# A two-layer trunk on one core: the dt chain moved to GpSimd, earlier tables, an opening with ones-matmuls, a split last half row

## The chip, the cores and the metric

One NeuronCore of one Trainium2 chip runs the whole program; the other cores are idle. The metric is the device time of one execution, in microseconds. The kernel before takes 1440.32 us (median of 3 runs, 1438.73 to 1442.22).

## The reference, cut to what matters

512 tokens of width 1024, float32, two layers. Each layer is a token mixer and a gated ConvFFN, both followed by a LayerNorm of `alpha*x + f(x)`. The mixer of layer 0 is a Mamba-2 scan, that of layer 1 a chunked spatial gate. The change touches the beginning of the scan and the very last LayerNorm:

```
zxbcdt = x @ w_in;  z, xbc, dt = split(zxbcdt)
xbc = silu(causal_dwconv(xbc));  xs, B, C = split(xbc)          # 8 groups, 4 heads each
dt = softplus(dt + dt_bias);  A = -exp(a_log);  Acum = cumsum(dt*A)
y_diag = sum_j (C_i.B_j) exp(Acum_i - Acum_j) dt_j x_j          # j <= i
states = sum_j B_j exp(Acum_last - Acum_j) dt_j x_j
out = layer_norm(alpha*x + conv_ffn(x))                         # the end of layer 1
```

## The kernel before, in words

Every float32 product is made of three matmuls in a rounded format: each operand is split into a rounded high part (a cast on ScalarE, ACT) and a low part (a subtraction on VectorE, DVE); the products high-high, high-low and low-high are summed in PSUM. The weights are one list `wall` of 244 tiles of 128x1024; `w_prep` (L74 to L85) loads each over the SP queue, casts it (L80) and subtracts (L82), six tiles ahead of its use. A projection tile of 128 channels by 512 tokens takes 24 matmuls of 512 columns, `mm_k` (L123 to L128), three for each of 8 blocks k of 128 input channels.

**Opening (L102 to L147).** The loop goes over k in pairs. For each k it loads a 256 KB block of x transposed (L136), casts it (L137) and subtracts (L138); for each pair it loads 256 columns of the first two weight tiles in 128 KB pieces (`w_piece`, L107 to L112); then it issues six matmuls, three into each of `ps_b[0]` and `ps_b[1]`, the first two channel tiles. That is 16 transfers. After them come `wdt` and the parameter table `ppt` (L144, L145) and the dt projection `dt_mm` into `ps_dt` (L119).

**The dt chain (L342 to L363).** One 128x128 tile (4 token blocks by 32 heads on the partitions, 128 tokens along the row) goes through the softplus by a polynomial, the product with exp(a_log), and a running sum S (the scan, L357). ACT does the exponentials, DVE the rest, one dependent instruction after another. S is written to DRAM (`scr`, L359) and read back broadcast to all partitions, for one group of four heads at a time (`R`, L377). `dt_cols` (L365 to L369) transposes three results on TensorE (PE) into `ptdt` and copies them to `tcol`; it is called when the matmuls of projection tile j=4, the first of group 1, have been issued.

**A group (L374 to L456).** `ssd(g, cv)` is a generator; `advance` (L460) calls its next part at each projection tile. Its first part loads R, issues the products C.B into `pcb`, the transposes of B (`pb`) and of x (`px`) on PE, then on ACT the decay tables `cd`, `E` (16 Relu, one Exp) and `EB`, and after them the copy `btok` of the transposed B (L409). Its second part issues the state products `pst` (L429), which read `btok`. For group 0 the first part is called after tile j=6 and the second after j=7.

**The end (`out_proj`, from L205).** The output projection sums 22 k-blocks into eight banks `acc[t][h]` (four row tiles t, two halves h of 512 columns). The last 5 k-blocks are done row tile by row tile (`tail`, half by half), so that each row tile's LayerNorm (`stats`, L252) runs while the next one's matmuls do. In `stats` DVE adds the residual (L259), takes the sums of 512 columns (L260) for each half, merges them (L261); GpSimd (POOL) takes the power -1/2 (L203); DVE scales, and SP writes out.

**What sets the order.** Instructions are written in the order of the source, each engine runs its own queue in a fixed order, and a planner (Tile) lays out the queues ahead of time by dependencies, priorities and a cost estimate, and puts in the semaphores. `tc.high_priority()` puts what is inside ahead. A queue stops at its first instruction that has to wait. PSUM has eight banks (`pst`).

Of the kernel before, what the change touches and what calls it, by code (L numbers as in the profile page):

```python
# [14 lines left out]
P = 128  # L15
T = 512
# [33 lines left out]
LOOK = 6  # L50


@with_exitstack
def trunk_kernel(ctx, tc, x_tok, x_t, w_dt, wall, pp, ln_g, ln_b, b_v, b_s, w_s_t, out):
# [52 lines left out]
    def w_piece(i, q):  # L107
        raw, hi, lo = first[i]
        cs = slice(q * 256, (q + 1) * 256)
# [20 lines left out]
    with tc.tile_pool(name="xload", bufs=8) as xl:  # L130
        wdt = xl.tile([P, NK, 32], F32, name="wdt", bufs=1)
        xr = []
        for q in range(4):
            for k in (2 * q, 2 * q + 1):
                xr.append(xl.tile([P, T], F32, tag="xr", name=f"xr{k}"))
                nc.sync.dma_start(xr[k], x_t[:, k, :])  # L136
                nc.scalar.copy(xT_hi[:, k, :], xr[k])  # L137
                nc.vector.tensor_sub(xT_lo[:, k, :], xr[k], xT_hi[:, k, :].bitcast(F32))  # L138
                if k % 2 == 0:
                    w_piece(0, q)  # L140
                    w_piece(1, q)
                for ps, f in zip(ps_b, first):
                    mm_k(ps, f[1:], k, 0, T)
# [61 lines left out]
    def out_proj(lnp, split, base, nk, ln, last, hooks=None, nxt=None, mid=None):  # L205
# [4 lines left out]
        def mm(t, h, k, a, w):  # L210
            o = acc[t][h]
            ts_ = slice(t * P, (t + 1) * P)
            hs = slice(h * T, (h + 1) * T)
            nc.tensor.matmul(o, a[0][:, ts_], w[0][:, hs], start=(k == 0), stop=False)  # L214
            nc.tensor.matmul(o, a[0][:, ts_], w[1][:, hs], start=False, stop=False)  # L215
            nc.tensor.matmul(o, a[1][:, ts_], w[0][:, hs], start=False, stop=(k == nk - 1))  # L216
# [28 lines left out]
        def tail(t):  # L245
            order = [(h, k) for h in range(2) for k in range(nm, nk)]
            if t == NT - 1 and not last:
                order = [(h, k) for k in range(nm, nk) for h in range(2)]
            for h, k in order:
                mm(t, h, k, *aw[k - nm])  # L250

        def stats(t):  # L252
            r = lnp.tile([P, D], F32, tag="r", bufs=2, name=f"r{base}_{t}")
            st = block(lnp, 12, f"st{base}_{t}", "st", 2).rearrange("p (a b) -> p a b", a=2)
# [70 lines left out]
    with ExitStack() as st:  # L325
# [16 lines left out]
        nc.scalar.activation(v, ps_dt[:, 0:P], AF.Identity, bias=col(C_DT))  # L342
        nc.vector.scalar_tensor_tensor(u, v, -1.0, v, ALU.mult, ALU.min)
        nc.scalar.activation(u, u, AF.Exp)
        nc.scalar.activation(ea, col(C_DT + 1), AF.Exp)
        nc.vector.tensor_scalar_add(q, u, 2.0)
        nc.vector.reciprocal(q, q)
        nc.vector.tensor_mul(u, u, q)
        nc.vector.tensor_mul(s2, u, u)
        nc.vector.tensor_scalar_mul(q, s2, 1.0 / 13.0)  # L350
        for c in (11, 9, 7, 5, 3):
            nc.vector.scalar_tensor_tensor(q, q, 1.0 / c, s2, ALU.add, ALU.mult)
        nc.vector.scalar_tensor_tensor(q, q, 1.0, u, ALU.add, ALU.mult)
        nc.vector.tensor_scalar_max(v, v, 0.0)
        nc.vector.scalar_tensor_tensor(v, q, 2.0, v, ALU.mult, ALU.add)
        nc.vector.tensor_scalar_mul(u, v, ea)
        nc.vector.tensor_tensor_scan(S, ones, u, 0.0, ALU.mult, ALU.add)  # L357
        for c in range(NT):
            nc.sync.dma_start(scr[:, c * P:(c + 1) * P], S[32 * c:32 * c + 32, :])  # L359
        nc.vector.tensor_scalar_mul(nsl, S[:, P - 1:P], -1.0)  # L360
        nc.scalar.activation(t4, S, AF.Exp, bias=nsl)
        nc.vector.tensor_mul(t4, t4, v)
        nc.vector.tensor_scalar_mul(u, S, -1.0)  # L363
# [10 lines left out]
        def ssd(g, cv):  # L374
            Bt, Ct, x0, x1 = (cv[:, i, :] for i in range(4))
# [4 lines left out]
            cd = small[:, 32 + 16 * (g % 2):48 + 16 * (g % 2)].rearrange("p (h c) -> p h c", h=4)  # L380
            pcb = pst(f"pcb{g}")
# [15 lines left out]
            nc.scalar.activation(cd, R[:, :, P - 1::P], AF.Exp, scale=-1.0)  # L397
            E = gp.tile([P, NT, 4, P], F32, tag="E", bufs=1, name=f"E{g}")
            for c in range(NT):
                for h in range(4):  # L400
                    nc.scalar.activation(
                        E[:, c, h, :], R[:, h, c * P:(c + 1) * P], AF.Relu,
                        bias=tcol[:, 0, c, 4 * g + h:4 * g + h + 1])
            nc.scalar.activation(E, E, AF.Exp, scale=-1.0)
            for h in range(2):
                hs = slice(64 * h, 64 * h + 64)
                nc.scalar.activation(EB[hs], R[hs, h::2, P:], AF.Exp, scale=-1.0)
# [353 lines left out]
```

## Time and profile before

| | |
|---|---|
| median of 3 runs | 1440.32 us |
| the profiled execution's own time | 1439.39 us |
| its span (first to last instruction) | 1437.5 us |
| PE busy | 1423.6 us (99%), 6911 matmuls and transposes |
| DVE, ACT, POOL busy | 846.1, 611.5, 23.7 us |
| DMA | 152.66 MB, mean 106 GB/s |

Times in the rows are from the start of the span. The span and the execution's time differ by 1.9 us, and the profiled execution is 0.9 us under the median. A matmul's row shows a modelled end, longer than the distance to the next one's start; the pace of a stream is the distance between starts.

### The profile page before, as it was taken

The page shows a single profiled execution, that of the slowest core. Times are in us where ns is not written, and L with a number is a line of the kernel's source. Part 1 is how long each engine was busy: PE and PEld are TensorE (multiplying, and loading weights), DVE is VectorE, ACT ScalarE, POOL GpSimd, SP SyncE. Part 2 cuts the span into 40 slices and gives each one's busy share as a digit, 9 for nine tenths or more (in the row PEclk, how much of TensorE's full clock was granted, in tenths as well). Part 3 has the DMA queues.
Part 4 walks back from the last instruction along what each step waited for, and adds up shares of the span by engine and source line. Part 5 has one row for each costly group of instructions (what it writes and reads, how often), then busy time and mean ns, then how long its engine had stood idle before and what let it go on. Part 6 is the DMA issues. An engine that isn't in the chain of part 4 may idle for free.

```text
span 1437.5 us, 17317 instructions
## 1 busy us (share of the span) xinstructions
PE 1423.6 (99%) x6911; PEld 1187.8 (83%) x6911; DVE 846.1 (59%) x1147; ACT 611.5 (43%) x893; POOL 23.7 (2%) x30
## 2 busy tenths in 40 slices
PE   8999999999999999999999999999999999999997
PEld 6788888888889888888888888888888888888886
DVE  6878777565378655554336556446378655554336
ACT  5886677343245433333233433223255433333220
POOL 0000000000000000000000000000000000000001
PEclk9999999999999999999999999999999999999999
DMA  6533322333424332323331432223223333333311
GB/s 219 206 106 129 106 100 74 88 115 122 160 73 123 112 99 92 103 90 101 93 98 59 154 125 88 88 88 118 89 81 127 101 103 93 98 103 118 103 44 59
DMA packets 42864, 152.66 MB, mean 106 GB/s; under 512 B 4760, under 2 KB 6040, under 8 KB 41504
## 3 DMA queue, kind: packets, MB, share of 16 engines
q1 hardware_dynamic: 40240, 143.17, 31.0%
q10 hardware_dynamic: 2544, 8.39, 1.7%
q8 instruction: 54, 0.88, 0.2%
q14 instruction: 26, 0.21, 0.0%
HBM read 149.37 MB, written 2.18 MB: 105 GB/s over the span
## 4 chain that ended last, share of the span: by engine, by line
PE 96%; ACT 1%; DVE 1%; DMA 1%; issue 0%; SPq 0%; DVEq 0%; ACTq 0%
PE ip L126 18%; PE ip L127 18%; PE ip L128 18%; PE acc L216 10%; PE acc L214 10%; PE acc L215 10%; PE pv L576 2%; PE pv L578 2%; PE pv L577 2%; PE psp L636 1%; PE py L443 1%; PE pt L279 1%; PE po L450 1%; PE pst L429 1%; PE pcb L384 0%; PE px L395 0%
## 5 line engine op out<-in xcount | busy, mean ns | idle before, releaser
L126 PE MATMUL ip<-xT_hi,whi 128*128 128x512 f32 (+1 forms) x1264 | 484.4, 383 | 0.0
L128 PE MATMUL ip<-xT_hi,wlo 128*128 128x512 f32 (+1 forms) x1264 | 479.8, 380 | 0.0
L127 PE MATMUL ip<-xT_lo,whi 128*128 128x512 f32 (+1 forms) x1264 | 478.7, 379 | 0.0
L82 DVE TENSOR_TENSOR wlo<-wraw,whi 128x1024 fp32r<-128x1024 f32 x242 | 295.7, 1223 | 297.8 <-ACT whi L80 297.3
L80 ACT CAST whi<-wraw 128x1024 fp32r<-128x1024 f32 x242 | 253.8, 1051 | 355.8 <-PE ip L127 289.3
L126 PEld LDWEIGHTS ip<-xT_hi,whi 128*128 128x128 f32 x1264 | 237.9, 188 | 45.3 <-issue 1.2
L128 PEld LDWEIGHTS ip<-xT_hi,wlo 128*128 128x128 f32 x1264 | 237.7, 188 | 44.6
L127 PEld LDWEIGHTS ip<-xT_lo,whi 128*128 128x128 f32 x1264 | 238.0, 188 | 43.3 <-issue 0.2
L214 PE MATMUL acc<-whi,ahi 128*128 128x512 f32 x608 | 237.3, 390 | 0.0
L216 PE MATMUL acc<-whi,alo 128*128 128x512 f32 x608 | 236.6, 389 | 0.0
L215 PE MATMUL acc<-wlo,ahi 128*128 128x512 f32 x608 | 236.5, 389 | 0.0
L214 PEld LDWEIGHTS acc<-whi,ahi 128*128 128x128 f32 x608 | 114.1, 188 | 24.2 <-issue 0.8
L216 PEld LDWEIGHTS acc<-whi,alo 128*128 128x128 f32 x608 | 114.1, 188 | 23.7
L215 PEld LDWEIGHTS acc<-wlo,ahi 128*128 128x128 f32 x608 | 114.1, 188 | 23.6
L193 DVE TENSOR_TENSOR alo<-h,ahi 128x512 fp32r<-128x512 f32 x44 | 30.4, 691 | 103.4 <-ACT ahi L192 103.4
L192 ACT CAST ahi<-h 128x512 fp32r<-128x512 f32 x44 | 27.4, 623 | 141.7 <-PE acc L215 119.5
L180 DVE SCALAR_TENSOR_TENSOR cv<-ip,ppt,cv 128x511 f32<-128x511 f32 (+2 forms) x90 | 66.9, 744 | 2.0 <-ACT cv L178 1.9
L180 DVE SCALAR_TENSOR_TENSOR gt<-ip,ppt,gt 128x511 f32<-128x511 f32 x88 | 65.7, 746 | 1.6 <-ACT gt L178 0.3
L180 DVE SCALAR_TENSOR_TENSOR ut<-ip,ppt,ut 128x511 f32<-128x511 f32 x88 | 65.7, 746 | 1.3
L563 ACT ACTIVATE gt<-gt 128x512 f32<-128x512 f32 x44 | 27.8, 632 | 82.6 <-DVE gt L180 82.5
L284 ACT ACTIVATE xf<-pt,ppt 128x128 f32<-128x128 f32 x96 | 36.6, 466 | 46.0 <-PE pt L279 43.6
L576 PE MATMUL pv<-whi,xT_hi 128*128 128x512 f32 x128 | 50.0, 390 | 0.0
(138 smaller groups left out, 1073.9 us busy)
## 6 DMA issues: line engine op xcount, KB each, us to landing
wraw<-in_wall_dram SPq DMA_DIRECT2D x242, 512.0 KB
xres<-scr SPq DMA_DIRECT2D x8, 1024.0 KB
xr<-in_x_t_dram SPq DMA_DIRECT2D x8, 256.0 KB
xres<-rscr SPq DMA_DIRECT2D x2, 1024.0 KB
xres<-in_x_tok_dram ACTq DMA_DIRECT2D x1, 2048.0 KB
out_dram<-r SPq DMA_DIRECT2D x8, 256.0 KB
wraw_s<-in_wall_dram SPq DMA_DIRECT2D x8, 128.0 KB
lngf<-in_ln_g_dram ACTq DMA_DIRECT2D x2, 512.0 KB
```

What stands on the lines that cost most here:

```text
L80: nc.scalar.copy(hi, raw)
L82: nc.vector.tensor_sub(lo, raw, hi.bitcast(F32))
L126: nc.tensor.matmul(o, whi[:, cs], xT_hi[:, k, lo:hi], start=(k == 0), stop=False)
L127: nc.tensor.matmul(o, whi[:, cs], xT_lo[:, k, lo:hi], start=False, stop=False)
L128: nc.tensor.matmul(o, wlo[:, cs], xT_hi[:, k, lo:hi], start=False, stop=(k == NK - 1))
L180: nc.vector.scalar_tensor_tensor(o[:, s:], ps[:, :T - s], col(c + taps - 1 - s), o[:, s:], ALU.mult, ALU.add)
L193: nc.vector.tensor_sub(lo, self.act(k), hi.bitcast(F32))
L214: nc.tensor.matmul(o, a[0][:, ts_], w[0][:, hs], start=(k == 0), stop=False)
L215: nc.tensor.matmul(o, a[0][:, ts_], w[1][:, hs], start=False, stop=False)
L216: nc.tensor.matmul(o, a[1][:, ts_], w[0][:, hs], start=False, stop=(k == nk - 1))
L284: nc.scalar.activation(xf[:, q, :], pt[:, q * P:(q + 1) * P], AF.Identity, scale=col(c), bias=col(c + 8))
L576: nc.tensor.matmul(ps, xT_hi[:, k, ts_], whi, start=(k == 0), stop=False)
```

## The change

- **Ones-matmuls.** Seven matmuls of the 128x128 tile of ones with itself, into `ps_dt`, stand ahead of the opening. Nothing reads their result.
- **Opening.** x arrives as blocks 0 and 1 (256 KB each) and then three pairs of 512 KB; the first two weight tiles come in pieces of 256, 256 and 512 columns. 11 transfers in place of 16, the same bytes.
- **dt chain.** 17 instructions leave DVE; 18 on POOL lead to the scan and three follow it. The reciprocal and the scan stay on DVE. The first exponent is now `exp(-|.|)` on ACT from PSUM. All of it has high priority.
- **Tables.** `decay(g)`, the load of R and the tables, is a function; for group 0 it is called right after `dt_cols`. In `ssd` the copy `btok` stands ahead of the tables.
- **Last half row.** For the last row tile of the last projection, half h=1 is computed as two pieces of 256 columns (30 matmuls in place of 15), and its residual and sums are taken in two pieces; the sums of this row tile are all taken over 256 columns.

```diff
+WARM = 7
+    pieces = {0: slice(0, 256), 2: slice(256, 512), 4: slice(512, 1024)}
+    for i in range(WARM):
+        nc.tensor.matmul(ps_dt[:, 0:P], ones, ones, start=True, stop=True)
...
+        xall = xl.tile([P, NK, T], F32, name="xall", bufs=1)
+        for k in range(NK):
+            xr.append(xall[:, k, :])
+            if k < 2:
                 nc.sync.dma_start(xr[k], x_t[:, k, :])
+            elif k % 2 == 0:
+                nc.sync.dma_start(xall[:, k:k + 2, :], x_t[:, k:k + 2, :])
+            nc.scalar.copy(xT_hi[:, k, :], xr[k])
+            nc.vector.tensor_sub(xT_lo[:, k, :], xr[k], xT_hi[:, k, :].bitcast(F32))
+            if k in pieces:
+                for i in range(2):
+                    w_piece(i, pieces[k])
+            for ps, f in zip(ps_b, first):
+                mm_k(ps, f[1:], k, 0, T)
...
+            if t == NT - 1 and last:
+                for h, c0, c1 in ((0, 0, 512), (1, 0, 256), (1, 256, 512)):
+                    for k in range(nm, nk):
+                        mm(t, h, k, *aw[k - nm], c0, c1)
+                return
...
             for h in range(2):
-                nc.vector.scalar_tensor_tensor(r[:, hs], xres[:, t, hs], ALPHA, acc[t][h], ALU.mult, ALU.add)
-                nc.vector.bn_stats(st[:, h, :], r[:, hs])
+                for c in ((0, 256) if short and h else (0,)):
+                    n = T // 2 if short and h else T
+                    nc.vector.scalar_tensor_tensor(
+                        r[:, h * T + c:h * T + c + n], xres[:, t, h * T + c:h * T + c + n], ALPHA,
+                        acc[t][h][:, c:c + n], ALU.mult, ALU.add)
+                    if short:
+                        for b in range(c // 256, (c + n) // 256):
+                            nc.vector.bn_stats(st[:, 2 * h + b, :], r[:, h * T + 256 * b:h * T + 256 * b + 256])
...
+        with tc.high_priority():
+            nc.scalar.activation(u, ps_dt[:, 0:P], AF.Abs, bias=col(C_DT))
+            nc.scalar.activation(u, u, AF.Exp, scale=-1.0)
+            nc.scalar.activation(v, ps_dt[:, 0:P], AF.Identity, bias=col(C_DT))
+            nc.scalar.activation(ea, col(C_DT + 1), AF.Exp)
+            gs.tensor_scalar_add(q, u, 2.0)
+            nc.vector.reciprocal(q, q)
+            gs.tensor_scalar_max(v, v, 0.0)
+            gs.tensor_tensor(u, u, q, ALU.mult)
+            gs.tensor_tensor(s2, u, u, ALU.mult)
+            gs.tensor_scalar(q, s2, 1.0 / 13.0, 1.0 / 11.0, ALU.mult, ALU.add)
+            for c in (9, 7, 5, 3):
+                gs.tensor_tensor(q, q, s2, ALU.mult)
+                gs.tensor_scalar_add(q, q, 1.0 / c)
+            gs.tensor_tensor(q, q, s2, ALU.mult)
+            gs.tensor_scalar(q, q, 1.0, 2.0, ALU.add, ALU.mult)
+            gs.tensor_tensor(q, q, u, ALU.mult)
+            gs.tensor_tensor(v, v, q, ALU.add)
+            gs.tensor_scalar_mul(u, v, ea)
+            nc.vector.tensor_tensor_scan(S, ones, u, 0.0, ALU.mult, ALU.add)
...
+            gs.tensor_scalar_mul(nsl, S[:, P - 1:P], -1.0)
+            nc.scalar.activation(t4, S, AF.Exp, bias=nsl)
+            gs.tensor_scalar_mul(u, S, -1.0)
+            gs.tensor_tensor(t4, t4, v, ALU.mult)
...
             btok = gp.tile([P, 3, P], F32, tag="btok", bufs=1, name=f"btok{g}")
             nc.scalar.copy(btok, pb[:, 0:384].rearrange("p (c n) -> p c n", c=3))
+            EB, cd, E = decays.pop(g) if g in decays else decay(g)
...
                 if g == 1 and k == 0:
                     dt_cols()
+                    decays[0] = decay(0)
```

## Rows read from the trace of the kernel before

**Rows 1.** The page's part 4: who holds the chain that ended last.
```profile
PE 96%; ACT 1%; DVE 1%; DMA 1%; issue 0%; SPq 0%; DVEq 0%; ACTq 0%
```
**Rows 2.** Waits of PE, whole run: who waited for whom, us, times, longest.
```profile
PE pst L429 <- ACT btok L409: 0.6, 1, 0.6
PE ptdt L368 <- DVE xres L363: 0.5, 1, 0.5
```
**Rows 3.** Timeline of PE's opening: start, us, instruction [idle before <-releaser].
```profile
4.71 0.80 PE L126 MATMUL ps_b<-xT_hi,whi_s 128*128 128x512 f32 x1 [4.71 <-ACT whi_s L111]
8.12 0.80 PE L126 MATMUL ps_b<-xT_hi,whi_s 128*128 128x512 f32 x1 [0.49 <-ACT xT_hi L137]
9.44 0.63 PE L128 MATMUL ps_b<-xT_hi,wlo_s 128*128 128x512 f32 x1
12.43 0.63 PE L126 MATMUL ps_b<-xT_hi,whi_s 128*128 128x512 f32 x1
13.53 0.40 PE L126 MATMUL ps_b<-xT_hi,whi_s 128*128 128x512 f32 x1
20.12 0.39 PE L128 MATMUL ps_b<-xT_hi,wlo_s 128*128 128x512 f32 x1
20.43 1.96 PE L119 MATMUL ps_dt<-xr,wdt 128*32 128x128 f32 x64
```
**Rows 4.** Timeline of the opening on DVE, ACT and SP.
```profile
0.90 0.17 DVE L102 MEMSET ones<- 128x128 f32 x1 [0.90 <-PEq L750]
7.45 1.39 ACT L137 CAST xT_hi<-xr 128x512 fp32r<-128x512 f32 x2 [2.08 <-DMA xr<-in_x_t_dram]
7.45 1.09 SPq L136 DMA_DIRECT2D xr<-in_x_t_dram  x2
14.44 0.62 ACT L137 CAST xT_hi<-xr 128x512 fp32r<-128x512 f32 x1 [1.02 <-DMA xr<-in_x_t_dram]
```
**Rows 5.** Timeline of the dt chain, its first and last steps.
```profile
22.46 0.37 ACT L342 ACTIVATE xres<-ps_dt,ppt 128x128 f32<-128x128 f32 x1 [0.20 <-PE ps_dt L119]
23.99 0.94 DVE L347 RECIPROCAL xres<-xres 128x128 f32<-128x128 f32 x1
38.03 0.42 DVE L357 TENSOR_TENSOR_SCAN xres<-ones,xres 128x128 f32<-128x128 f32 x1
39.43 0.41 PE L368 MATMUL ptdt<-ident,xres 128*128 128x128 f32 x2 [0.50 <-DVE xres L363]
```
**Rows 6.** Groups of POOL, whole run: count | busy us, mean ns | idle before.
```profile
L203 POOL TENSOR_TENSOR rs<-rs,small 128x1 f32<-128x1 f32 x16 | 12.8, 802 | 989.3 <-DVE rs L202 989.3
masks.py:199 POOL TENSOR_SCALAR_AFFINE_SELECT ident<-ident 128x128 f32<-128x128 f32 x1 | 0.3, 292 | 0.1
```
**Rows 7.** Timeline of group 0's tables on ACT and its state product on PE.
```profile
50.16 0.23 ACT L397 ACTIVATE small<-xres 128x16 f32<-128x16 f32 x1 [1.49 <-DMA xres<-scr]
58.51 0.48 ACT L409 COPY btok<-pb 128x384 f32<-128x384 f32 x1
59.04 1.13 PE L429 MATMUL pst<-xw,btok 128*128 128x256 f32 x4 [0.57 <-ACT btok L409]
```
**Rows 8.** Timeline around the first transposes of the first output projection.
```profile
409.89 1.03 PE L279 MATMUL pt<-ident,xres 128*128 128x128 f32 x8
410.52 1.15 ACT L284 ACTIVATE xf<-pt,ppt 128x128 f32<-128x128 f32 x3 [10.27 <-PE pt L279]
```
**Rows 9.** Timeline of DVE after the last matmul.
```profile
1430.02 0.69 DVE L259 SCALAR_TENSOR_TENSOR r<-xres,acc 128x512 f32<-128x512 f32 x1 [1.10 <-PE acc L216]
1430.74 0.69 DVE L260 BATCH_NORM_STATS2 st<-r 128x6 f32<-128x512 f32 x1
```
**Rows 10.** Instructions 256 columns wide: PE's timeline, and a DVE group.
```profile
430.45 0.28 PE L128 MATMUL ip<-xT_hi,wlo 128*128 128x256 f32 x1
432.96 0.28 PE L128 MATMUL ip<-xT_hi,wlo 128*128 128x256 f32 x1
L436 DVE TENSOR_TENSOR hst<-hst,pst 128x256 f32<-128x256 f32 x16 | 6.6, 415 | 0.0
```

More of the change, by code (lines that the diff above doesn't have):

```diff
@@ L105, in trunk_kernel, with w_piece @@
               for tag, dt_, n in (("wraw", F32, 3), ("whi", F32R, WB), ("wlo", F32R, WB))] for i in range(2)]
-    def w_piece(i, q):
+    pieces = {0: slice(0, 256), 2: slice(256, 512), 4: slice(512, 1024)}
+    def w_piece(i, cs):
         raw, hi, lo = first[i]
-        cs = slice(q * 256, (q + 1) * 256)
         nc.sync.dma_start(raw[:, cs], wall[i][:, cs])
@@ L128, in mm_k @@
         nc.tensor.matmul(o, wlo[:, cs], xT_hi[:, k, lo:hi], start=False, stop=(k == NK - 1))
-    with tc.tile_pool(name="xload", bufs=8) as xl:
+    with tc.tile_pool(name="xload", bufs=1) as xl:
         wdt = xl.tile([P, NK, 32], F32, name="wdt", bufs=1)
         xr = []
-        for q in range(4):
-            for k in (2 * q, 2 * q + 1):
-                xr.append(xl.tile([P, T], F32, tag="xr", name=f"xr{k}"))
+        xall = xl.tile([P, NK, T], F32, name="xall", bufs=1)
+        for k in range(NK):
+            xr.append(xall[:, k, :])
+            if k < 2:
                 nc.sync.dma_start(xr[k], x_t[:, k, :])
[L137 to L143, printed above, removed]
+            elif k % 2 == 0:
[7 more added lines that the diff above has]
+                mm_k(ps, f[1:], k, 0, T)
         nc.sync.dma_start(wdt, w_dt)
@@ L208, in out_proj, with mm @@
         acc = [[pst(f"acc{base}_{t}_{h}") for h in range(2)] for t in range(NT)]
-        def mm(t, h, k, a, w):
-            o = acc[t][h]
+        def mm(t, h, k, a, w, c0=0, c1=T):
+            o = acc[t][h][:, c0:c1]
             ts_ = slice(t * P, (t + 1) * P)
-            hs = slice(h * T, (h + 1) * T)
+            hs = slice(h * T + c0, h * T + c1)
             nc.tensor.matmul(o, a[0][:, ts_], w[0][:, hs], start=(k == 0), stop=False)
             nc.tensor.matmul(o, a[0][:, ts_], w[1][:, hs], start=False, stop=False)
-            nc.tensor.matmul(o, a[1][:, ts_], w[0][:, hs], start=False, stop=(k == nk - 1))
+            nc.tensor.matmul(o, a[1][:, ts_], w[0][:, hs], start=False, stop=(k == nk - 1 and c1 == T))
         k0 = 0
@@ L253, in stats @@
             r = lnp.tile([P, D], F32, tag="r", bufs=2, name=f"r{base}_{t}")
-            st = block(lnp, 12, f"st{base}_{t}", "st", 2).rearrange("p (a b) -> p a b", a=2)
+            st = block(lnp, 24, f"st{base}_{t}", "st", 2).rearrange("p (a b) -> p a b", a=4)
+            short = last and t == NT - 1
+            if not short:
+                st = st[:, 0:2, :]
             mv = block(lnp, 2, f"mv{base}_{t}", "mv", 2)
@@ L341, in trunk_kernel @@
         nsl = small[:, 17:18]
[L342 to L363, printed above, removed]
+        gs = nc.gpsimd
+        with tc.high_priority():
[18 more added lines that the diff above has]
+            nc.vector.tensor_tensor_scan(S, ones, u, 0.0, ALU.mult, ALU.add)
+            for c in range(NT):
+                nc.sync.dma_start(scr[:, c * P:(c + 1) * P], S[32 * c:32 * c + 32, :])
+            gs.tensor_scalar_mul(nsl, S[:, P - 1:P], -1.0)
+            nc.scalar.activation(t4, S, AF.Exp, bias=nsl)
+            gs.tensor_scalar_mul(u, S, -1.0)
+            gs.tensor_tensor(t4, t4, v, ALU.mult)
@@ L372, in trunk_kernel, with decay @@
         gp = pool(st2, "ssmg")
-        def ssd(g, cv):
-            Bt, Ct, x0, x1 = (cv[:, i, :] for i in range(4))
+        decays = {}
+        def decay(g):
             R = xsl[:, 4 * (g % 2):4 * (g % 2) + 4, :]
@@ L380, in ssd @@
             cd = small[:, 32 + 16 * (g % 2):48 + 16 * (g % 2)].rearrange("p (h c) -> p h c", h=4)
+            nc.scalar.activation(cd, R[:, :, P - 1::P], AF.Exp, scale=-1.0)
+            E = gp.tile([P, NT, 4, P], F32, tag="E", bufs=1, name=f"E{g}")
+            for c in range(NT):
+                for h in range(4):
+                    nc.scalar.activation(
+                        E[:, c, h, :], R[:, h, c * P:(c + 1) * P], AF.Relu,
+                        bias=tcol[:, 0, c, 4 * g + h:4 * g + h + 1])
+            nc.scalar.activation(E, E, AF.Exp, scale=-1.0)
+            for h in range(2):
+                hs = slice(64 * h, 64 * h + 64)
+                nc.scalar.activation(EB[hs], R[hs, h::2, P:], AF.Exp, scale=-1.0)
+            return EB, cd, E
+        def ssd(g, cv):
+            Bt, Ct, x0, x1 = (cv[:, i, :] for i in range(4))
             pcb = pst(f"pcb{g}")
```

13 lines of the change are left out of this document (2 added, 11 removed).

## The prediction, as it was put on record

> **What bounds the kernel now.** I read the page's chain first: 96% of it is PE [rows 1]. So a step is worth what it takes out of PE's own stream, or what it takes off the two ends where PE has no matmul: the opening, and the LayerNorm behind the last one. Then I asked for PE's waits over the whole run. Beside those of the opening there are two, of 0.5 and 0.6 us [rows 2], and both lie in stretches that the change touches. A wait in that view starts at the modelled end of the matmul before, 0.39 us after its start, while the stream's pace is 0.227 us; so each costs PE 0.16 us more: 0.66 (`ptdt`) and 0.73 us (`pst`).
>
> Then the timeline of the opening. The first matmul starts at 4.71 us, when its weights have been cast [rows 3]. The second x block is cast at 7.45, after ACT stood 2.08 us for its transfer [rows 4], and PE goes on at 8.12. From 9.44 to 12.43 there are seven steps, 0.427 us each: 512 columns in that time is the lower of the clock's two levels, 1.2 GHz. From 13.53 to 20.12 there are 29 steps of 0.227 us, the upper level [rows 3]. What PE did before the rise: work from 4.71, a gap before 8.12, and then work without a gap. The page's clock line, in slices of 36 us, does not show this; the pace does. At the other end DVE takes the residual and sums, 0.72 us from start to start, straight behind the last matmul [rows 9].
>
> **The change part by part, against the profiled execution's own 1439.39 us; the sum is then put on the median, 0.93 us above.**
>
> *Ones-matmuls.* The tile of ones is written at 1.07 us [rows 4]; until 4.71 PE has nothing else, so they cost nothing if they end by then. The nearest row is eight 128-column transposes in 1.03 us [rows 8], 0.13 each at the upper level, so 0.26 at the lower, and twice that if a full float32 product takes two passes: 1.8 to 3.6 us for seven, ending between 2.9 and 4.7. What they can give: PE has then worked from 1.1 us on, with short gaps, and the clock may rise before 8.12 in place of 13.3. The gain is 0.2 us for each of the 12 matmuls between 8.12 and 13.3, 2.4 us; at the other end it is nothing, if the clock rises when it did.
>
> *Opening transfers.* The bytes are the same. Between the casts at 7.45 and 14.44 [rows 4] six x blocks and six weight pieces come in, 2304 KB in 7.0 us, or 0.78 us for 256 KB. A pair is complete 0.78 us after its first block would have been; PE has block 1 to work on (1.4 us at the upper level) from 8.12, so part of that is covered. I take +0.4, between 0 and +0.8. Five transfers less on SP could be worth something: SP issued the next x block only at 7.45 [rows 4]. But the transfers on which the path depends then, x blocks 0 and 1 and the first pieces, are issued in the same order as before; I take 0 for it and keep the rest for a rival. A check from the other side: the last pair lands at about 14.4 as before, two casts (1.39), one subtraction more (about 0.7) and six matmuls (1.4) give 17.9; PE by its own pace from 8.12 ends its 42 matmuls at 8.12 + 9.5 + 0.5 for waits = 18.1, and 18.4 or so with the pairs. Before it was 20.43. So the opening gives -2.0, bounds 0 and -2.4, and all that follows is 2.0 us earlier. The weight stream is loaded six tiles ahead and follows.
>
> *dt chain.* Before: first step at 22.46, the scan at 38.03 [rows 5], 15.6 us for a chain in which DVE puts other work between the steps. `ptdt` waited for its end, 0.66 us. After: `ps_dt` is done at 22.39 - 2.0 = 20.4; 0.7 for two activations, 17 POOL steps on the chain (the maximum lies beside the reciprocal), 0.94 for the reciprocal [rows 5], 0.42 for the scan and about 1.0 for DVE's queue, twice: S at 23.5 + 17p. The trace has no POOL arithmetic on a 128x128 tile. Its nearest row is a one-input select of the same size, 0.29 us; the far one is the power on one column, mean 0.80 [rows 6]. That gives S at 28.4 or 37.1. I take p = 0.45, nearer the row with the same size and half more for a second input: 31.2. Behind S come two more POOL steps and an exponential for the third transposed tile, 32.6. Before, PE was through with tile j=4 at 39.43 - 0.66 = 38.77 [rows 5], now at 36.8, so the wait of 0.66 goes, with 4 us to spare. What is behind the chain in the queues: ACT's casts of weight tiles 3 to 5 are not due before PE is three tiles on; SP's four writes of S and the load of R come earlier, and weight loads queue behind R while it waits for them, some 2 us against a lead of six tiles of 5.4 us (24 x 0.227). The 17 instructions less on DVE are off the path and count nothing. Bounds: -0.66, and at p = 0.80 a wait of 2.4 in place of 0.66, +1.8.
> On this the Trainium skill, page "GPSIMD Engine Reference", section 4.1 Engine selection, speaks against the move: it has VectorE about twice as fast for elementwise work with two inputs. Its 4497 ns for 2048 elements would make, as my estimate from that page, 0.28 us for 128 columns without the fixed part. No row here shows such an instruction, and the sum above does not use this.
>
> *Tables for group 0, B copied ahead.* R arrived at 50.16, 11.7 us after S; ACT then made tables until 58.51, and the copy of B stood behind them, so PE waited until 59.04 [rows 7]. After: S at 31, R by 43, tables (8.3 us) by 51.5, the copy due before 59.04 - 0.6 - 2.0 - 0.7 = 55.7. The wait of 0.73 goes, with 4 us to spare; if R comes no earlier against PE than before, it stays, 0. The convolutions of tiles j=4 and 5 come behind the tables on ACT and hold two PSUM banks longer; with the five of group 0's products that is seven of eight, so I cost it at nothing, and a bank too few would show as a wait of `pcb`.
>
> *Last half row.* The 30 matmuls of 256 columns: 21 steps in 432.96 - 430.45 = 2.51 us [rows 10], 0.1195 each, 3.59 us against 15 x 0.227 = 3.41: +0.18. Then DVE. A 256-column instruction from PSUM takes 0.415 us [rows 10] against 0.69 [rows 9], with 0.03 between. If the first piece is read while PE writes the second, only two short ones are left behind the last matmul: 0.89 in place of 1.44, -0.55. If not, four are: up to 1.78, +0.34. Which one? The first copy out of a `pt` bank reads only the first of four transposes, which start 0.11 apart from 409.89 and last 0.27, so it was free at 410.16; ACT had been idle for 10 us, and started at 410.52 [rows 8], when the fourth was done at 410.48. So a reader waits for all that has been written to its bank before it in the source, and here all 30 matmuls stand ahead of `stats`. I take +0.27 for DVE, since the second residual need not wait for the first sums: +0.45 in all, bounds -0.37 and +0.52.
> The Trainium skill, page "PSUM — Partial Sum Buffer", section PSUM bank collisions raise a hardware error, speaks against this part as well: two engines in the same bank at once, also in different columns, are an error, which software has to keep apart. By that rule the trace agrees: the 0.36 us by which ACT started late [rows 8].
>
> **The sum.** -2.0 - 0.66 - 0.73 + 0.45 = -2.94 us. On the profiled execution 1436.4, on the median 1440.32 - 2.94 = 1437.4 us. Unknowns by their bounds: opening 0 to -2.4, chain -0.66 to +1.8, tables 0 to -0.73, last row -0.37 to +0.52.
>
> **The rivals.**
> 1. *The clock rises when it did.* PE stays full of gaps until 8.12, and before it also stayed low after work with a gap. Then the opening gives 0: 1440.32 - 0.94 = 1439.4 us. Against it: PE would have worked most of the time from 1.1 us.
> 2. *The second x block lands earlier.* Its 2.08 us of waiting on ACT are not explained by the bytes ahead of it alone (768 KB by 7.45, against 2304 KB in the 7 us behind). With fewer transfers it could come 1.5 us earlier, and with the clock up all that follows too: 1435.9 us. Against it: the same four transfers stand ahead.
> 3. *The last half row overlaps* after all: -0.37 in place of +0.45, 1436.6 us. Against it [rows 8].
> 4. *POOL is late, and the kernel slower.* One mechanism: `ptdt` stands in PE's fixed order behind tile j=4, and every microsecond by which the chain is late there is lost. The third tile is ready at 24.0 + 19p, PE at 36.8; the loss equals all gains, 2.94, at p = 0.83. With the power's mean of 0.80 and 0.15 from one dependent step to the next, p = 0.95, the wait is 5.3 us, and the sum -2.0 - 0.66 + 5.3 - 0.73 + 0.45 = +2.4: 1442.7 us. For it: the only POOL arithmetic in the trace costs that [rows 6]. Against it: that is a power, and a select of the full tile takes 0.29.
>
> The rule of the skill's GPSIMD page is why this rival has 8% and not less.
>
> **How the numbers follow.** Forecast 47%, rivals 1 to 4: 20, 15, 10 and 8%. About 0.2% (2.9 us) is what a measurement of this kernel can tell from no change; below 1437.4 counts as faster. Faster: somewhat over half of the forecast (26), rival 2 (15) and most of rival 3 (8), 49%. Slower: rival 4 and 3 of the rest, 11%. Within: 40%. Range: from 1434.6 (rival 2 with the last row's better end) to 1440.8 (rival 1 with a wait left, or rival 4 at its mildest). The forecast's own range is 1436.3 to 1438.5, from the opening's and the last row's bounds.
>
> **What would show it.** Opening: matmuls of `ps_b` at 0.227 us from 8.12 on or before, and the first `ps_dt` at 18.4; if the pace is 0.427 until 13, rival 1. Chain: POOL's 128x128 steps between 0.3 and 0.6 us, the scan near 31, and no wait of `ptdt` among PE's waits; a wait there of over 2.9 us would make the whole wrong. Tables: no wait of `pst` for `btok`. End: from the last matmul to the first merge of the sums 1.7 us in place of 1.45; if it is 0.9, the pieces overlap. The rest of PE's stream, 40 to 1430 us, should be the same to within 0.3 us; a new wait there would be an effect of the planner's new order that I have not priced.

## The result, and the profile after

The changed kernel takes 1448.20 us (median of 5 runs, 1447.56 to 1449.17) against 1440.32 before: ratio 1.0056, 95% interval 1.0044 to 1.0067. It is slower by 8 us, or 0.6%, where 2.9 us of gain were forecast. Its profiled execution took 1448.24 us, span 1446.5. In the chain that ended last PE still holds 96%, as in [rows 1].

The ledger first: when PE started the same instruction, in both timelines, in us from the span's start.

| PE starts | before | after | difference |
|---|---|---|---|
| last matmul of `ps_b` (opening) | 20.12 | 19.11 | -1.0 |
| first transpose into `ptdt` | 39.43 | 37.77 | -1.7 |
| first `pst` of group 0 | 59.04 | 62.48 | +3.4 |
| first `py` of group 0 | 66.01 | 74.52 | +8.5 |
| last matmul of all | 1429.59 | 1438.52 | +8.9 |
| end of the span | 1437.5 | 1446.5 | +9.0 |

So 10 us are lost between 38 and 75 us, and nothing to speak of behind that. PE's waits in the kernel after say where:

```profile
PE pst L464 <- ACT btok L443: 5.5, 1, 5.5
PE pst L464 <- ACT hst L467: 1.5, 1, 1.5
PE ps_b L131 <- ACT xT_hi L145: 1.0, 1, 1.0
```

The wait of `ptdt` is gone, as forecast. The wait of `pst` for `btok`, which was to go too, has grown from 0.6 [rows 2] to 5.5 us. PE's own timeline shows the stop, and what it costs beyond itself:

```profile
56.54 0.39 PE L133 MATMUL ip<-xT_hi,wlo 128*128 128x512 f32 x1
62.48 1.22 PE L464 MATMUL pst<-xw,btok 128*128 128x256 f32 x2 [5.55 <-ACT btok L443]
65.16 2.56 PE L464 MATMUL pst<-xw,btok 128*128 128x256 f32 x4 [1.46 <-ACT hst L467]
67.15 0.99 PE L131 MATMUL ip<-xT_hi,whi 128*128 128x512 f32 x1
67.94 0.63 PE L132 MATMUL ip<-xT_lo,whi 128*128 128x512 f32 x1
68.36 0.63 PE L133 MATMUL ip<-xT_hi,wlo 128*128 128x512 f32 x1
```

Behind the stop the matmuls start 0.43 us apart (67.94, 68.36), the lower level of the clock; from 71 us on it is 0.23 again. A third stop is hidden in the second row: its four matmuls are two pairs, and the second pair starts at 66.49 only, behind DVE's product `xw` for it (66.02, below). In the chain that ended last it is this stop that stands, behind ACT's tables. To find why the copy `btok` was late, go back along the queue of ACT, which made it (timeline of ACT, after):

```profile
27.09 0.78 ACT L186 ACTIVATE cv<-ip,ppt 128x512 f32<-128x512 f32 x1 [3.22 <-PE ip L133]
37.10 0.40 ACT L390 ACTIVATE xres<-xres,small 128x128 f32<-128x128 f32 x1 [9.23 <-POOL small L389]
37.41 1.99 ACT L81 CAST whi<-wraw 128x1024 fp32r<-128x1024 f32 x2
...
48.54 0.47 ACT L398 COPY tcol<-ptdt 128x384 f32<-128x384 f32 x1
49.02 1.28 ACT L411 ACT_TABLE_LOAD   x1
50.38 0.23 ACT L411 ACTIVATE small<-xres 128x16 f32<-128x16 f32 x1
...
57.85 0.84 ACT L421 ACTIVATE EB<-xres 64x768 f32<-64x768 f32 x1
58.72 0.78 ACT L186 ACTIVATE cv<-ip,ppt 128x512 f32<-128x512 f32 x1
59.40 1.03 ACT L81 CAST whi<-wraw 128x1024 fp32r<-128x1024 f32 x1
60.33 0.78 ACT L186 ACTIVATE cv<-ip,ppt 128x512 f32<-128x512 f32 x1
61.01 1.04 ACT L81 CAST whi<-wraw 128x1024 fp32r<-128x1024 f32 x1
61.94 0.48 ACT L443 COPY btok<-pb 128x384 f32<-128x384 f32 x1
```

ACT stood 9.23 us. Its next instruction was the exponential at the end of the dt chain (L390), which waits for POOL, and the casts of weights behind it, whose data were there, could not pass. From 37 us on ACT runs behind: `ptdt` was done by 38.4, but its copy to `tcol` starts at 48.54 only, and the tables at 50.38, no earlier than before (50.16, [rows 7]). The tables could not start sooner for another reason too, which lies on SP (its wait and its timeline, after):
```profile
SPq L388 <- DVE xres L386: 8.4, 1, 8.4
```
```profile
41.76 1.72 SPq L407 DMA_DIRECT2D xres<-scr  x1
```
SP stood 8.4 us for the scan, before it could write S. Behind the writes three weight loads stand ahead of the load of R in its queue, and the last of them waits for DVE's late subtractions (38.88 to 41.23). So R leaves at 41.76, as before (41.75), though S was ready 1.7 us earlier; in the chain that ended last it lands at 50.35, when ACT has just loaded its function table (50.30). After the tables two convolutions and two casts stand ahead of `btok`, which is copied at 61.94 in place of 58.51. DVE shows the same stop, in front of the scan; a second one at 57.86, where it waits 6.88 us for the tables with `xw` and other work behind it; and then the end of the kernel:

```profile
25.34 3.79 DVE L83 TENSOR_TENSOR wlo<-wraw,whi 128x1024 fp32r<-128x1024 f32 x3
36.32 0.42 DVE L386 TENSOR_TENSOR_SCAN xres<-ones,xres 128x128 f32<-128x128 f32 x1 [7.20 <-POOL xres L385]
...
57.86 0.69 DVE L473 TENSOR_TENSOR E<-E,cbm 128x512 f32<-128x512 f32 x1 [6.88 <-ACT E L418]
...
66.02 0.41 DVE L453 TENSOR_TENSOR xw<-px,tcol 128x256 f32<-128x256 f32 x1
...
1438.83 0.75 DVE L277 SCALAR_TENSOR_TENSOR r<-xres,acc 128x256 f32<-128x256 f32 x2 [1.23 <-PE acc L224]
1439.50 0.74 DVE L282 BATCH_NORM_STATS2 st<-r 128x6 f32<-128x256 f32 x2
1440.28 0.26 DVE L285 BATCH_NORM_AGGREGATE mv<-st 128x2 f32<-128x24 f32 x1
```

What POOL was doing meanwhile (its timeline, after):

```profile
24.95 0.46 POOL L375 TENSOR_TENSOR xres<-xres 128x128 f32<-128x128 f32 x1 [1.07 <-DVE xres L373]
25.48 1.33 POOL L376 TENSOR_TENSOR xres<-xres 128x128 f32<-128x128 f32 x1
26.91 1.15 POOL L377 TENSOR_SCALAR xres<-xres 128x128 f32<-128x128 f32 x1
28.14 1.31 POOL L379 TENSOR_TENSOR xres<-xres 128x128 f32<-128x128 f32 x1
29.54 0.53 POOL L380 TENSOR_SCALAR xres<-xres 128x128 f32<-128x128 f32 x1
...
35.67 0.62 POOL L385 TENSOR_SCALAR xres<-xres,small 128x128 f32<-128x128 f32 x1
```

From 29.54 to 35.67 there are eleven steps in 6.13 us, 0.56 each. The three between 25.48 and 29.45 take two to three times as long, and lie beside DVE's three subtractions of 25.34 to 29.13. The busy times of the same nine microseconds close the picture (windows: PE, PEld, DVE, ACT, POOL busy us, granted clock, share of the DMA engines, GB/s), first after, then before:

```profile
28.00:37.00 9.00, 9.00 (x41) 7.46 (x40) 1.80 (x3) 0.00 (x0) 7.34 (x15) 1.00 0.29 110
57.00:67.00 10.00, 2.95 (x5) 1.50 (x6) 9.09 (x14) 9.10 (x13) 0.00 (x0) 0.67 0.51 164
```
```profile
29.00:38.00 9.00, 9.00 (x41) 7.45 (x40) 8.72 (x15) 3.94 (x4) 0.00 (x0) 1.00 0.73 239
```

PE is full in both, fed from the six tiles prepared ahead. But 6.9 us of DVE's work, 3.9 of ACT's and more than half of the transfers did not happen. The bill comes at 57 us, where DVE and ACT are 91% busy and PE 30%.

### The profile page after: what moved, and what is told of

It reads as the page before. It is cut to its first block, busy times and chain, and to the rows that moved or that the text cites. A ratio compares the mean times of both kernels' runs of the same rounds, so it can differ in the third digit from the quotient of the medians.

```text
span 1446.5 us, 17365 instructions
## 1 busy us (share of the span) xinstructions
PE 1428.3 (99%) x6940; PEld 1191.6 (82%) x6940; DVE 843.0 (58%) x1131; ACT 610.8 (42%) x892; POOL 36.1 (2%) x51
## 4 chain that ended last, share of the span: by engine, by line
PE 96%; ACT 2%; DMA 1%; DVE 1%; issue 0%; SPq 0%; DVEq 0%; ACTq 0%
PE ip L131 18%; PE ip L132 18%; PE ip L133 18%; PE acc L222 10%; PE acc L223 10%; PE acc L224 10%; PE pv L612 2%; PE pv L614 2%; PE pv L613 2%; PE py L478 1%; PE psp L672 1%; PE pt L303 1%; PE pst L464 1%; ACT E L415 1%; PE po L485 1%; DMA xres<-scr 1%
## 5 line engine op out<-in xcount | busy, mean ns | idle before, releaser
L222 PE MATMUL acc<-whi,ahi 128*128 128x512 f32 (+1 forms) x613 | 238.2, 389 | 0.0
L224 PE MATMUL acc<-whi,alo 128*128 128x512 f32 (+1 forms) x613 | 237.5, 387 | 0.0
L223 PE MATMUL acc<-wlo,ahi 128*128 128x512 f32 (+1 forms) x613 | 237.4, 387 | 0.0
L308 ACT ACTIVATE xf<-pt,ppt 128x128 f32<-128x128 f32 x96 | 36.7, 467 | 45.6 <-PE pt L303 43.6
```

Source lines behind the costliest of these rows:

```text
L308: nc.scalar.activation(xf[:, q, :], pt[:, q * P:(q + 1) * P], AF.Identity, scale=col(c), bias=col(c + 8))
```

## The experiments

Each run stands beside runs of the kernel before on the same chip (median 1439.3 to 1440.0 us). Theory Q says that ACT, DVE and SP stand behind the end of the chain on POOL, and that this is the loss. Rival E blames the early tables, rival P the speed of POOL's arithmetic wherever it is put. In every run with the chain on POOL its arithmetic keeps the high priority that the change gave it; POOL without the priority was not run, so what of the loss is due to the priority is open.

**e1: the change with the chain as it was, on DVE.**
```diff
-        gs = nc.gpsimd
-        with tc.high_priority():
...
+        nc.vector.scalar_tensor_tensor(u, v, -1.0, v, ALU.mult, ALU.min)
```


> The changed kernel with the dt chain as it was before (DVE, one step after another, no priority); opening, early tables, B copied ahead and the split last half row stay. Theory Q (fixed queues): in the changed kernel the last steps of the POOL chain (scan on DVE, exponential on ACT, four writes on SP) stand in their queues ahead of other work, long before POOL is through; ACT, DVE and SP stand 9, 7 and 8 us, and the backlog delays the tables and the copy of B that PE then waits for. Without the POOL chain none of that is left: no wait of ACT over 4 us between 20 and 40 us, no wait of pst for btok over 0.3 us, and 1439.0 us (1438.3 to 1440.0), from the opening's -1.0, pst's -0.7 and the last row's +0.4. Rival E (early tables): it is the call of the tables ahead of the convolutions that delays the copy of B; then pst still waits 4 us or more here, and the time is 1444 to 1448.


Measured: 1442.25 us, ratio 1.0020 (1.0010 to 1.0029). The long stops are gone, so E falls, and the chain's move is worth 5 to 6 of the 8 us. But the time is 2 us above Q's bound. PE's waits:
```profile
PE ptdt L392 <- DVE xres L387: 1.9, 1, 1.9
PE pst L459 <- ACT btok L438: 0.9, 1, 0.9
```
Against [rows 3, 5] the opening was 1.8 us earlier in this trace (last `ps_b` at 18.36), the end of the chain only 0.3 (`ptdt` at 39.09), so PE waits for `ptdt` instead; behind the stop some matmuls run at the lower level. What an earlier opening is worth is taken up below.

**e2: the change without the early tables of group 0.**
```diff
-                    decays[0] = decay(0)
```


> The changed kernel without the early call: group 0's tables are made in its own place again, B still copied ahead. Theory Q: ACT, DVE and SP still stand behind the chain's last steps until about 36 to 37 us (9, 7, 8 us), so the backlog is still there and PE still loses at group 0's products: 1442 to 1448 us. Rival E: without the early call the time falls to 1438.5 to 1440.


Measured: 1446.55, ratio 1.0050 (1.0035 to 1.0065). ACT stands 9.22 us and DVE 7.20 as in the change, and PE's stops at `pst` stay (3.3 and 2.3 us, now for `hst` and `xw`). Q holds. What the early tables cost, some 1 us, is within the uncertainty.

**e3: the change, with the chain's end tied to the convolution of tile j=3.** The scan reads a tile of ones that is computed from that convolution's result, so the planner cannot put the scan, the exponential and the writes of S ahead of it.
```diff
-            nc.vector.tensor_tensor_scan(S, ones, u, 0.0, ALU.mult, ALU.add)
+        def chain_end(o):
+            nc.vector.tensor_scalar(ones2, o[:, 0:P], 0.0, 1.0, ALU.mult, ALU.add)
+            nc.vector.tensor_tensor_scan(S, ones2, u, 0.0, ALU.mult, ALU.add)
...
+                if g == 0 and k == 3:
+                    chain_end(cv[:, k, :])
```


> The changed kernel with POOL's arithmetic as it is, but the chain's end (scan, four writes, exponential and what follows) made dependent on the convolution of tile j=3, by one 128x128 DVE instruction that makes the scan's ones out of it; so the planner has to lay the weight casts, the subtractions and two convolutions ahead of the scan. Theory Q: DVE and SP no longer stand over 3 us for POOL, weight transfers go on between 28 and 37 us, and the time is 1438.5 to 1441. A rival P (POOL's arithmetic is too slow wherever its end stands, or slows DVE): PE waits at ptdt or pst as before, 1445 to 1448. Under Q a part may come back if POOL's steps lengthen while DVE works beside them: those beside a 128x1024 subtraction took 1.15 to 1.33 us in the changed kernel, those beside an idle DVE 0.46 to 0.53.


Measured: 1444.48, ratio 1.0033 (1.0022 to 1.0045): between the two. The standstill and both stops at `pst` are gone, which is Q. But one new wait stands in PE's list, which is P; below it, POOL's rows of this run:
```profile
PE ptdt L402 <- POOL xres L396: 4.1, 1, 4.1
```
```profile
31.14 1.50 POOL L379 TENSOR_TENSOR xres<-xres 128x128 f32<-128x128 f32 x1
32.72 0.53 POOL L380 TENSOR_SCALAR xres<-xres 128x128 f32<-128x128 f32 x1
33.34 1.18 POOL L379 TENSOR_TENSOR xres<-xres 128x128 f32<-128x128 f32 x1
...
37.87 1.51 POOL L385 TENSOR_SCALAR xres<-xres,small 128x128 f32<-128x128 f32 x1
```
With DVE at work all the time seven of POOL's steps take 1.1 to 1.5 us, and the chain reaches the scan at 39.38; on DVE the scan itself was done by 38.45 [rows 5]. Of the 4.1 us another 1.2 are DVE's queue: a subtraction stands ahead of the scan, which starts at 40.59. Both Q and P are true, and each hides the other: in the kernel after POOL was quick because DVE stood waiting for it.

**e4: the kernel before with the chain on POOL alone.**
```diff
-        nc.vector.scalar_tensor_tensor(u, v, -1.0, v, ALU.mult, ALU.min)
...
+        gs = nc.gpsimd
+        with tc.high_priority():
```


> The kernel before with only the dt chain on POOL, with its priority; opening, tables, copy of B and last row as before. Theory Q: slower than before by 4 to 9 us (1444 to 1449), ACT, DVE and SP standing behind the chain's end. Rival E: 1439.5 to 1441, as the tables are not called early.


Measured: 1444.81, ratio 1.0038 (1.0023 to 1.0053). Without early tables and with the old opening the stops of `pst` for `btok` and of ACT are there again, and a wait at `ptdt` beside them:
```profile
PE pst L434 <- ACT btok L414: 4.8, 1, 4.8
PE ptdt L373 <- POOL xres L367: 1.5, 1, 1.5
```
```profile
37.91 0.40 ACT L366 ACTIVATE xres<-xres,small 128x128 f32<-128x128 f32 x1 [10.52 <-POOL small L365]
```

**e5, e6, e7: the opening, whole and in halves, in the kernel before.** e5 has both parts, e6 the ones alone, e7 the 11 transfers alone (WARM = 0).
```diff
+    for i in range(WARM):
+        nc.tensor.matmul(ps_dt[:, 0:P], ones, ones, start=True, stop=True)
```


> The kernel before with the change's opening alone: the matmuls of ones and the 11 transfers. In the kernel after, TensorE's last matmul of the opening's ps_b rows began at 19.11 us instead of 20.12, so the opening gives 1.0 us. Theory G (given back): the dt chain on VectorE ends when it ended, 39.4 us, so TensorE reaches ptdt 1.0 us sooner and waits there 1.3 to 2.0 us instead of 0.5; behind so long a stop the granted clock falls for some matmuls. Time 1439.0 to 1441, no gain. Rival K (kept): VectorE's chain also starts earlier by what the opening gains; ptdt waits 0.7 us or less, time 1438.0 to 1438.6.

> The kernel before with the seven matmuls of ones alone; its 16 transfers stay. Theory G: clock at the upper level from about 5.8 us instead of 13.3 (as the trace of the kernel after has it), the opening's last matmul 1 to 2 us earlier, the whole of it given back at ptdt (wait 1.5 to 2.5 us), time 1439.0 to 1441. Rival K: ptdt waits 0.7 or less, time 1437.4 to 1438.4, which would be the prediction's -2.0 for the opening.

> The kernel before with the 11 transfers alone, no matmuls of ones. If the transfers carry the opening's gain, its last matmul begins near 19.1 and the clock still rises late; if, as I read the trace after, the pairs of x land together and the second of a pair is no sooner while the first is later, the last matmul begins at 20.0 to 20.6 and the time is 1439.4 to 1440.2. Theory G says that no gain of either would be seen in the time in any case: not under 1439.0.


Measured: e5 1441.03, ratio 1.0012 (1.0003 to 1.0021); e6 1439.20, 0.9994 (0.9985 to 1.0003); e7 1441.05, 1.0004 (0.9995 to 1.0013). The transfers are no gain, and with the ones a small loss. e5 lies at the upper end of what G allows, and e7 0.85 us above its forecast. The third x block, the first that comes in a pair, is cast at 8.76 to 9.50 in the eight traces that have the pairs; as a block by itself it is cast in the pair of casts that starts at 6.80 (e6) or 7.45 [rows 4], and at 8.28 in e10. The ones bring the opening's last matmul to 17.41 in e6's trace, 2.7 us earlier than in [rows 3]; the time gains 0.9 us by the ratio, and its interval goes from a loss of 0.4 to a gain of 2.2. PE waits of e5, then e6:
```profile
PE ptdt L376 <- DVE xres L371: 2.2, 1, 2.2
PE pst L437 <- ACT btok L417: 2.0, 1, 2.0
```
```profile
PE ptdt L372 <- DVE xres L367: 1.4, 1, 1.4
```
Theory G's mechanism is there in both, and in e6 its size was overstated: the chain too came 1.3 us earlier (first `ptdt` at 38.09), and the last matmul of all 1.5 us (1428.08), so about half is kept.

**e8: the last half row in two pieces, alone.**
```diff
+                for h, c0, c1 in ((0, 0, 512), (1, 0, 256), (1, 256, 512)):
...
```


> The kernel before with the last half row in two pieces alone. In the trace after, the first of VectorE's two 256-wide pieces starts only behind the last matmul, and last matmul to merge takes 1.48 us against 1.49 before: VectorE's part is 0. TensorE issues 10 matmuls of 256 columns twice in place of 512 columns once, 30 more starts at +0.006 each: +0.18. Theory: 1439.4 to 1439.8. The prediction's term was +0.45 (1439.85). Rival: the first piece overlaps, -0.8 us, 1438.6.


Measured: 1440.06 against 1440.02, ratio 1.0002 (0.9993 to 1.0011). (It is 15 matmuls of 512 columns that become 30 of 256.) By its interval, -1.0 to +1.6 us, the time alone rules out neither the overlap's -0.8 nor +0.2 or +0.45; the overlap is ruled out by the trace, in which both pieces start behind the last matmul (1430.11) and the merge follows 1.49 us after its end, as before. By chance this trace tests G again. Its clock rose early without any ones (the `ps_b` matmuls start 0.23 us apart from 9.5 on, the last at 18.38, 1.7 us earlier than in [rows 3]), and its span is 1437.7 us against 1437.5:
```profile
PE ptdt L384 <- DVE xres L379: 2.9, 1, 2.9
```
Why did the chain not start earlier with PE? Its first step stands in ACT's queue behind a cast that had to wait for its weight tile until 19.94, and starts at 23.17, against 22.46 [rows 5].

**e9 to e12: a shorter chain.** If PE's stop at `ptdt` swallows the opening, a shorter chain on DVE must give it back. The polynomial is cut by two terms: alone (e9), with the ones (e10), and with B's copy ahead as well (e11); e12 is B's copy ahead alone.
```diff
-        nc.vector.tensor_scalar_mul(q, s2, 1.0 / 13.0)
-        for c in (11, 9, 7, 5, 3):
+        nc.vector.tensor_scalar_mul(q, s2, 1.0 / 9.0)
+        for c in (7, 5, 3):
```


> The kernel before with two steps fewer in VectorE's dt chain: the series of log1p stops at the term of 1/9 instead of 1/13 (two scalar_tensor_tensor of 0.28 us less; the output changes by the terms left out, at most about 1.5e-6 of dt). In the trace before one chain step stands behind each 1.22 us subtraction, so the end of the chain comes up to 2 x 1.3 us earlier, not 0.57. Theory G (TensorE's stop at ptdt takes up whatever the opening gives; what shortens the chain shortens the stop): there is only a 0.5 us wait to remove in the kernel before: time 0 to 0.6 us below before. Rival W (VectorE's amount of work from 20 to 44 us is the bound, not the chain's end): 0.57 us less work, ptdt waits as before, no gain either. The next run tells them apart.

> The matmuls of ones (as run alone: 1439.2 against 1440.0, with a 1.4 us wait at ptdt) and the chain shorter by two steps. Theory G: the wait at ptdt falls under 0.4 us and its time comes back: 1.0 to 2.2 us below before (1437.8 to 1439.0 if before is 1440.0). Rival W: the next wlo or whi that TensorE needs is late instead, the ptdt wait only changes its name, time as the ones alone, 0.4 to 0.9 us below before.

> As the run before it with B's copy also put ahead of the table loads. Group 0's pst waited 0.6 us for that copy in the kernel before, 0.2 with the ones alone. Theory: 0 to 0.6 us below the ones with the short chain, no pst wait over 0.3 us. Rival: the copy, 0.45 us on ScalarE, only pushes the Exps of E behind it, and the wait moves to the next reader (xw or E*cbm): same as the run before it or up to 0.5 us more.

> The kernel before with B's copy put ahead of the table loads, alone. The prediction counted 0.73 us for it. Theory: the 0.6 us wait of pst for btok goes, nothing else moves in group 0, time 0.3 to 0.8 us below before. Rival: the copy moves ahead in ScalarE's queue by 0.45 us of other work, what it passes is late by that, and the time is that of before within 0.3.


Measured: e9 1438.63, ratio 0.9990 (0.9982 to 0.9999), by its middle more than G gave it; e10 1437.92, 0.9986 (0.9977 to 0.9995), no wait at `ptdt`: G, not W; e11 1436.60, 0.9980 (0.9971 to 0.9988), **the best kernel here, by the ratio 2.9 us under before**, and 1.3 us under e10, where 0 to 0.6 was expected and the intervals overlap; e12 1438.98, 0.9997 (0.9988 to 1.0005). In e12 the wait of `pst` for `btok` is gone; the time may have moved by 0.4, which this doesn't show for certain. The first steps of e11 against [rows 5, 7]:
```profile
37.18 0.38 PE L372 MATMUL ptdt<-ident,xres 128*128 128x128 f32 x2
...
56.04 1.02 PE L433 MATMUL pst<-xw,btok 128*128 128x256 f32 x4
```
Neither row has a wait: PE is 2.2 us ahead at `ptdt` and 3.0 at `pst`, and its last matmul starts 2.8 us earlier than before. That the ones need the shorter chain is read from such waits; the times don't show it. Alone the ones gave 0.9 and the short chain 1.4 us, together 2.0, no more than their sum.

**e13: the change with the polynomial on POOL cut by the same two terms. e14: as e3, tied to tile j=2.**
```diff
-            gs.tensor_scalar(q, s2, 1.0 / 13.0, 1.0 / 11.0, ALU.mult, ALU.add)
-            for c in (9, 7, 5, 3):
+            gs.tensor_scalar(q, s2, 1.0 / 9.0, 1.0 / 7.0, ALU.mult, ALU.add)
+            for c in (5, 3):
```
```diff
-                if g == 0 and k == 3:
+                if g == 0 and k == 2:
```


> The kernel after with the series on GpSimd stopped at the term of 1/9: two multiplications and two additions fewer there, 2 x (0.46 + 0.53 and two gaps of 0.08 to 0.15) = 2.2 to 2.3 us (the output changes by the terms left out). Theory Q (ScalarE, VectorE and SyncE stand behind the end of the chain on GpSimd, and TensorE's stop at pst is that standstill passed on): ScalarE's wait of 9.2 us becomes about 7, the pst waits of 5.5 + 1.5 us become 3 to 5 in all, less of the stretch runs at the lower clock, and the time is 1443.5 to 1446.2. If the pst stop is not the standstill's child, the time stays at 1447.5 to 1448.5.

> The kernel after with the end of its chain made to depend on the convolution of tile j=2, where the run with j=3 had no standstill but 4.1 us at ptdt. Is there a place where the chain on GpSimd costs nothing? Rival P (the arithmetic on GpSimd ends too late wherever its end is put: 7 of its 18 steps took 1.1 to 1.5 us beside VectorE's subtractions and it ended at 39.4 us, no earlier than VectorE's own 39.4 before): some of both, VectorE and ScalarE stand 1 to 4 us, ptdt waits 1 to 4 us, time 1441.0 to 1444.5. Rival place (only the order was wrong): neither wait over 1 us, 1437.5 to 1439.5.


Measured: e13 1446.86, ratio 1.0047 (1.0033 to 1.0061). ACT's stop and the one at `pst` shrink as Q has it, but a wait of 1.3 us at `pcb` is new and the time is 0.7 us above Q's range; its interval overlaps that of the change itself. The stop is part of the chain of causes, and its length does not pass on one to one.
```profile
34.38 0.40 ACT L390 ACTIVATE xres<-xres,small 128x128 f32<-128x128 f32 x1 [6.95 <-POOL small L389]
```
```profile
PE pst L464 <- ACT btok L443: 4.1, 1, 4.1
PE pcb L429 <- ACT cv L513: 1.3, 1, 1.3
```
e14 1442.60, ratio 1.0021 (1.0012 to 1.0030), as P expects: a standstill on DVE (4.48 us) and on ACT (4.42), a little over the 4 us that P gave, and waits at `ptdt` as well, in PE's list:
```profile
PE ptdt L402 <- POOL xres L396: 1.6, 1, 1.6
PE ptdt L402 <- POOL xres L397: 1.1, 1, 1.1
```
Its time is that of e1, where the chain is on DVE (1.0020): at this place the move costs nothing that could be told, and gains nothing. Of the four places tried (the planner's in after and e4, j=2, j=3) none gives a gain.

The parts, each measured alone as 1440 times its ratio's excess: chain on POOL +5.5, opening +1.7, last half row +0.3, B ahead -0.4; the early tables, as after minus e2, +0.9. Sum +8.0, measured +8.1. Each carries 1.3 us of uncertainty or more (the chain 2.2, the tables 2.7), so that they meet to 0.1 us is chance; that the chain is the largest part is not.

## Why the prediction was wrong

**The step that failed** is the one on the chain's surroundings: "What is behind the chain in the queues", costed at nothing beyond SP's "some 2 us against a lead of six tiles". I looked for what PE would wait for, and asked of ACT's casts only when PE needs them. I did not ask how long ACT and DVE would stand *in front of* the chain's end. In the kernel before DVE stood at most 0.75 us at a time between 20 and 40 us, since the steps of the chain and the weights took turns in its own queue. With the steps on POOL, the scan and the exponential become waits across engines; the planner put only a convolution and three subtractions on DVE, and a cast and a convolution on ACT, between the start of the chain and its end, and the queues stop there for 7 and 9 us. Six tiles of lead covered PE at `ptdt`. They did not cover the later duties of ACT, DVE and SP. "R by 43, tables (8.3 us) by 51.5 ... with 4 us to spare" met an R that landed at 50.35, since SP's queue had stood too, tables that ended at 58.69, a `btok` copy at 61.94 and an `xw` at 66.02. R came no earlier than before, and ACT would not have been ready for it: both were the gate.

**The chain's step** (p = 0.45, S at 31.2) was too small: 0.56 us a step undisturbed, 0.71 on the mean of the 16 behind the reciprocal (24.95 to 36.29), S at 36.7. That `ptdt` stopped waiting was right, but by luck: not "with 4 us to spare", since the third tile was ready at 38.05 and PE came at 37.77, and only because DVE stood still for POOL. With DVE at work rival 4's price appears: 0.91 us a step in e3 (24.77 to 39.38) against its 0.95, and a wait of PE at `ptdt` of 4.1 us against its 5.3.
The steps that were long lie in the rows beside DVE's subtraction of two SBUF tiles (1.22 us); beside convolutions, which read one input from PSUM, they took 0.46 to 0.53 (e3, 29.36 to 31.05). The Trainium skill, page "SBUF — State Buffer", section Who interferes with whom, states this as a rule: a VectorE instruction with two SBUF inputs and a GpSimd instruction that reads SBUF exclude each other, and the second waits. The traces agree (1.09 to 1.51 us in place of 0.46 to 0.53), and it spoke against this change more than the rule that I had weighed.

**The opening** (-2.0) was mis-sized: -1.0 in the trace after, and no gain is left when more traces are counted. In the trace after PE's clock was up before 8.12, against rival 1; the second x block was cast at 7.29 against 7.45, against rival 2. But with the faster clock PE waits for x and the weights instead, and the pairs make that worse (the casts in e5 and e6). Also, the late rise on which the term rests is not a property of the kernel. Five traces have the old opening without ones: in two of them the `ps_b` matmuls are slow until 13 us and end at 20.12 and 20.16 (before, e12), in three they are fast by 9.5 and end at 18.10 to 18.38 (e4, e8, e9). The seven traces with the change's opening end at 18.36 to 20.24, no earlier; in two of these (e2, e5) the clock had risen and fell again behind the gap before the second x block. Only the three traces with ones and without pairs end earlier, at 17.41 to 18.05 (e6, e10, e11). And a part of an earlier opening is lost again at `ptdt`, where PE waits for the chain (1.4 us in e6, none in e10).

**B's copy ahead** (-0.73) removed its wait where the rest was left alone (e12); what that is worth in time, 0.4, is below what the runs resolve.

**The last half row** (+0.45): +0.18 on PE as worked out; on DVE 0 in place of +0.27. From the end of the last matmul to the merge it is 1.48 us (1438.80 to 1440.28), as before. Both pieces start behind the last matmul, so the reading of [rows 8] held: the reader waits for all the matmuls into its bank that stand ahead of it. Whether the planner's semaphores alone make it wait, no run shows. The four instructions of 256 columns took 1.41 us, not 1.78. Rival 3 falls with that.

**The 17 instructions less on DVE**, "off the path and count nothing": true in the change, but the waits at `ptdt` in e5, e6, e8 and e9 show that DVE's chain is on the path when PE comes early.

Two readings of the prediction don't hold by its own rows. The lower end of the range, 1434.6, is not "rival 2 with the last row's better end": 1435.9 - 0.82 is 1435.1. And [rows 6] is not the only arithmetic of POOL in the trace before: two powers on 128x16 (L492) took 2.9 us each. Neither changes what failed.

## What to carry to other kernels

Before moving a dependent chain to an idle engine, list for every engine that consumes its result what stands behind the consuming instruction in that engine's fixed queue, and for how long: the stop falls on all of it, and shows up tens of microseconds later as a wait for something unrelated. When a gain in one stretch goes missing, look for the next place where PE waits for another chain, and shorten that chain; here two polynomial terms less, at the price of a slightly different result, gave what an engine more did not. A term that rests on the clock of one profiled execution should be checked against other traces of the same instructions first.

## What the runs showed of the hardware

PE's clock fell to its lower level during the long stop and stayed there after work had resumed: the windows of the kernel after show a granted clock of 0.67 from 57 to 67 us and 0.55 in the next four, and the starts are 0.43 us apart until 70 us. From 67.94 to 70.50 six starts took 2.56 us in place of 6 x 0.227 = 1.36, so the stop cost at least 1.2 us beyond itself. The length of a stop alone did not decide this: behind 1.9 us (e1) and 4.1 us (e3) at `ptdt` there are starts 0.43 us apart, behind 2.2 us (e5) and 2.9 us (e8) none.

At the start of the kernel the rise to the upper level came at different times in executions with the same matmuls: by 9.5 us in e4, e8 and e9, after 13 us in before and e12.
